# VectorE's weight halves ordered behind the recurrence's outputs while the pooling branch runs, and three of four weight sums made inside the raw tiles

## Chip, cores, metric

One core of one Trainium2 chip runs the kernel. The metric is device time in microseconds (us) of one execution: the median of 3 runs before the change was 2531.32 us (2531.08 to 2533.26). Engines are written as in the profile: PE is TensorE (PEld its weight loads), DVE is VectorE, ACT is ScalarE, POOL is GpSimd, SP is SyncE, which here only issues DMAs.

## What is computed

One layer of a hybrid trunk over 2048 positions and 1024 channels, all in float32. Cut to what matters here:

```python
xn = rmsnorm(x, norm1_g)
z = xn @ w_in                                  # columns: pool | q | forget | input | output gate | branch gates
u_pool, zq, zf, zi, zo, zg = split(z)
gates = sigmoid(zg + b_gate)
ya = pool_mixer(u_pool) @ w_pa                 # trailing-window means, windows 2, 4, 8, 16
yb = hgrn2_mixer(zq, zf, zi, zo) @ w_pb        # S_t = f_t S_(t-1) + (1 - f_t) i_t ; o_t = S_t q_t
x = x + (gates[0] * ya + gates[1] * yb) @ w_o
x = x + conv_glu_ffn(rmsnorm(x, norm2_g))      # up, causal conv of width 3, SiLU gate, down
return rmsnorm(x, final_g)
```

## The kernel before

**Stages.** The sequence is worked in two superblocks of 1024 positions, each of two blocks of 512. For each superblock the kernel runs a mixer (the projections `io`, `fq`, `u` and `g`, then the pooling branch `pa`, the recurrence branch `pb`, and `wo`) and then the feed-forward part (`up`, `dn`). The first mixer ends some 626 us into the profile, the second runs from about 1276 us.

**Products.** A matrix product over two blocks of rows is made by a seven-product scheme of the Strassen kind: a "unit" (class `Unit`, L1161) is one 2x2 arrangement of weight quarters q0 to q3, multiplied in seven products P1, P6, P5, P7, P2, P4, P3 (`ORDER`, L50). Four of them need a sum of weight quarters: `SUM_OF` (L349) names s2 for P6, s1 for P5, s3 for P7 and s4 for P3. Products gather in three PSUM banks X, Z and V. Between P6 and P7, DVE must take u2 = e1 - Z out of bank Z (L1196), since P7 adds to Z again; between P7 and P4 it must take u3 = Z - e1 (L1200) for the same reason. PE waits at P7 or at P4 when that read is late.

**Weight halves.** Each product is made of three matmuls per 128 rows with a weight tile split in two: `convert` (L216) lets ACT round the tile to float32r (L231, "high half") and DVE subtract it from the original (L232, "low half"), both into an `ops` tile. Six ops tiles exist (`N_OPS`), so the halves of product j can be written only when product j - 6 is finished. The source is a raw tile (L192), of which there are eight (`N_RAW`), filled by a DMA that SP issues (L197).

**The sums.** In the first mixer `weights_of_unit` (L433) makes each unit's four sums on POOL (L444). Each goes to a tile of its own out of the 77 slots that all stages share (`slot`, L109), and `keep` (L332) has it stored to DRAM by SP (L341). The second mixer loads the stored sums (`sums_of_unit`, L423) and makes none. So the sums are made in the first mixer alone, for the 14 units of `PROJ` (L55): fq0, g0, u0, fq1, g1, g2, fq2, g3, u1, g4, fq3, g5, g6, g7.

**The recurrence.** `hgrn_task` (L965) runs beside the projections for 4 heads and 2 blocks. At its end DVE scales the output, `ot` (L1138, four parts), PE transposes it (L1144), ACT copies it (L1146), and it goes through DRAM to become an operand of `pb`. `ot` needs a row factor `ro` from POOL (L691). The last head's outputs fall into the time of the pooling branch.

**What sets the order.** The kernel emits instructions from one Python loop: every six matmuls a tick (L136) advances one conversion and the waiting tasks. The Tile scheduler then sets the order of each engine's instructions; `behind(a, b)` (L259) adds an ordering edge between two instructions of one engine, without a wait. `quiet[0]` is true from P1 of the last unit (L1482) to the end of the `pb` branch (L1563).

Of the kernel before, what the change touches and what calls it, by code (L numbers as in the profile page):

```python
# [18 lines left out]
P = 128  # L19
# [62 lines left out]
def tile_trunk(  # L82
# [16 lines left out]
    pe, act, dve, pool, sp = nc.tensor, nc.scalar, nc.vector, nc.gpsimd, nc.sync  # L99
# [9 lines left out]
    def slot(name, cols=TB, dt=F32):  # L109
        return slots.tile([P, cols], dt, tag="s", name=name, padded_shape=[P, 528])  # L110

    def bank(name, cols=512):
        return banks.tile([P, cols], F32, tag="b", name=name, padded_shape=[P, 512])

    def f32(ap):
        return ap.bitcast(F32)
# [5 lines left out]
    class Task:  # L122
        def __init__(self, gen):
            self.gen = gen
            self.wait = 0
            self.live = True
            tasks.append(self)
# [40 lines left out]
    class Stream:  # L168
        def __init__(self):
            self.raws = []  # L170
            self.ops = []
            self.n_raw = 0
            self.tiles = []
            self.next = 0
            self.done = 0
            self.pins = {}
            self.stop = None
            self.room = LOOKAHEAD

        def raw(self, src, plus=None):  # L180
            r = Raw(src, plus)
            self.raws.append(r)
            return r
# [32 lines left out]
        def convert(self):  # L216
            j = len(self.tiles)
            key, fn, raws = self.ops[j]
            while any(r.tile is None for r in raws):
                self.load()  # L220
            for r in raws:
                r.add()
            store_kept()
            v = fn(f"w{j}")
            t = opsp.tile([P, 2, 512], F32R, tag="ops", name=f"ops{j}")
            n = int(np.prod(v.shape[1:]))
            hi, lo = t[:, 0, :n], t[:, 1, :n]
            if len(v.shape) == 3:
                hi = hi.rearrange("p (a b) -> p a b", a=v.shape[1])
                lo = lo.rearrange("p (a b) -> p a b", a=v.shape[1])  # L230
            self.mark = act.copy(hi, v)  # L231
            low = self.low = dve.tensor_tensor(lo, v, f32(hi), ALU.subtract)  # L232
            if j in self.pins:
                for ins, other in zip((self.mark, low), self.pins[j]):
                    behind(ins, other)
            self.tiles.append((key, t))
            self.load_ahead()
# [21 lines left out]
    def behind(ins, other):  # L259

        tc.add_manual_dep(ins.ins, other.ins.name, mybir.DependencyInfo(
            mybir.DependencyClass.NoSync, mybir.DependencyReason.DATA), reason="behind")
# [17 lines left out]
    stream = Stream()  # L280
# [51 lines left out]
    def keep(key, t, later=False):  # L332

        nm = "kw" + "".join(str(c) for c in np.ravel(key[1])) + f"{key[0]}{key[2]}"
        kept[key] = dram.tile([P, 512], F32, tag=nm, name=nm)
        keeping.append((kept[key], t, later))

    def store_kept():
        while keeping:
            d, t, later = keeping.pop(0)  # L340
            ins = sp.dma_start(d, t)  # L341
            if later:
                behind(ins, stream.low)
# [5 lines left out]
    SUM_OF = {"P5": "s1", "P6": "s2", "P7": "s3", "P3": "s4"}  # L349
# [42 lines left out]
    def plan_unit(key, src, kind, i, order, b0):  # L392
        mv, mg = proj_tiles(kind, i)
        if b0:
            unit = sums_of_unit(src, mv, mg, lambda p: lambda: kept["in", (kind, i), SUM_OF[p]])
        else:
            unit = weights_of_unit(src[mv], src[mg], (kind, i))
        for p in order:
            fn, raws = unit[p]()
            stream.op(key, fn, raws)  # L400
# [19 lines left out]
    def quarters(src_v, src_g):  # L420
        return [s[:, c * 512 : (c + 1) * 512] for s in (src_v, src_g) for c in range(2)]
# [10 lines left out]

    def weights_of_unit(src_v, src_g, unit):  # L433
        src = quarters(src_v, src_g)
        raws, tmp = {}, {}

        def raw(i):
            if i not in raws:
                raws[i] = stream.raw(src[i])
            return raws[i]  # L440

        def comb(nm, key, x0, x1):
            t = slot(f"{nm}{key}")
            pool.tensor_tensor(t, x0, x1, ALU.add)  # L444
            tmp[key] = t
            keep(("in", unit, key), t)
            return t

        def plan(p):
            if p == "P5":  # L450
                return (lambda nm: tmp["s1"]), []
            rs = [raw(i) for i in {"P1": (0,), "P2": (1,), "P4": (3,), "P6": (0, 2, 3),
                                   "P7": (0, 2), "P3": (1,)}[p]]

            def fn(nm):
                t = [r.tile for r in rs]
                if p == "P6":
                    comb(nm, "s1", t[1], t[2])
                    return comb(nm, "s2", tmp["s1"], t[0])
                if p == "P7":  # L460
                    return comb(nm, "s3", t[1], t[0])
                if p == "P3":
                    return comb(nm, "s4", tmp["s2"], t[0])
                return t[0]

            return fn, rs

        return {p: (lambda p=p: plan(p)) for p in ORDER}

    def up_order():  # L470
# [40 lines left out]
    prep, quiet = [], [False]  # L511
# [176 lines left out]
    def rstd_of(ssq, n, scale, name):  # L688
        r = small.tile([P, 4], F32, tag="rstd", name=name)
        pool.tensor_scalar(r[:, :n], ssq, scale, EPS, ALU.mult, ALU.add)  # L690
        pool.tensor_tensor(r[:, :n], r[:, :n], neghalf[:, :n], ALU.pow)  # L691
        return r
# [272 lines left out]
    def hgrn_task(b, h, d, q, vd, zd, od):  # L965
        def head_of(src, key):
# [14 lines left out]
        q1, q2 = (slot(f"q{i}{b}_{h}").rearrange("p (c s x) -> p c s x", c=NT, s=2)  # L981
                  for i in (1, 2))
# [68 lines left out]
        for lv in (0, 1, 2, 4, 6):  # L1051
# [35 lines left out]
            q3 = q.rearrange("p (b t h) -> p b t h", t=2, h=hh)  # L1087
# [34 lines left out]
        po = bank(f"po{b}_{h}")  # L1122
# [11 lines left out]
        r = rstd_of(so, NT, 1.0 / P, f"ro{b}_{h}")  # L1134
        yield 4
        ot = slot(f"ot{b}_{h}")
        for c in range(NT):
            dve.scalar_tensor_tensor(ot[:, c * P : (c + 1) * P], po[:, c * P : (c + 1) * P],  # L1138
                                     r[:, c : c + 1], zt[:, c * P : (c + 1) * P],
                                     ALU.mult, ALU.mult)  # L1140
        yield 4
# [3 lines left out]
        t = slot(f"oh{b}_{h}")  # L1145
# [221 lines left out]
    def mixer(b0, forms, late):  # L1367
# [16 lines left out]
        def runner():  # L1384
            while taken[0] < 2 * HEADS:
                if queue:
                    taken[0] += 1
                    yield from hgrn_task(*queue.pop(0))
                else:
                    yield 1  # L1390
# [487 lines left out]
```

## Time and profile before

| | |
|---|---|
| median of 3 runs | 2531.32 us (2531.08 to 2533.26) |
| the profiled execution, its own time | 2530.39 us |
| its span, first to last instruction | 2528.7 us |
| mean granted PE clock | 0.999 |
| busy: PE, DVE, ACT, POOL | 2507.8, 1963.1, 1195.1, 746.3 us |

The span is 1.7 us shorter than the execution's own time. Rows of the profile name an instruction by engine, line of the kernel, operation and tiles as out<-in without buffer numbers: `ops<-raw` is a weight half made from a raw tile, `gr_Z` is bank Z of a gate unit, `fr_` and `ur_` those of the forget/query and pooling units, `gr_u` a u2 or u3. Rows of time begin with the start in us from the span's start and the duration in us; a bracket at the end is the engine's idle time before the row and what ended it. In a row of a stretch each engine has its busy time and its number of instructions.

### The profile page before, as it was taken

The numbers are of one execution on the slowest core, as the hardware profiler recorded it, in microseconds if no ns is written. First come the engines' busy times: TensorE is split into PE (matmuls) and PEld (weight loads), VectorE is DVE, ScalarE is ACT, GpSimd is POOL, SyncE is SP. The second block draws the span as 40 slices with busy tenths as digits, with TensorE's granted clock in tenths as the row PEclk, the third lists the DMA queues.
The fourth block names the chain that finished last, engine by engine and source line by source line (L and its number), as shares of the span: only waits on it lengthen the run. The fifth ranks groups of instructions, "written<-read, shape, count | busy, mean of one in ns | idle before, by whom it ended". The sixth has DMA issues, their size and how long they took to land.

```text
span 2528.7 us, 35641 instructions
## 1 busy us (share of the span) xinstructions
PE 2507.8 (99%) x11508; PEld 2053.8 (81%) x11508; DVE 1963.1 (78%) x3476; ACT 1195.1 (47%) x2250; POOL 746.3 (30%) x1127
## 2 busy tenths in 40 slices
PE   9999999999999999999999999999999999999998
PEld 7888888788888888888888888888888888888887
DVE  7788878598898777885596778665979988778755
ACT  6534443334555454554554444542355554445534
POOL 4333453003354334451320202200033432325410
PEclk9999999999999999999999999999999999999999
DMA  8877777777898879997344343447443454447852
GB/s 272 271 184 231 203 203 231 221 230 244 200 259 231 229 230 240 265 364 244 123 150 150 109 134 109 138 148 233 140 155 118 151 153 135 153 133 245 321 166 97
DMA packets 252331, 493.75 MB, mean 195 GB/s; under 512 B 26544, under 2 KB 43056, under 8 KB 251824
## 3 DMA queue, kind: packets, MB, share of 16 engines
q1 hardware_dynamic: 184512, 313.60, 39.2%
q0 software_dynamic: 42656, 112.74, 17.5%
q10 hardware_dynamic: 24976, 65.13, 7.5%
q8 instruction: 91, 1.49, 0.2%
q14 instruction: 96, 0.79, 0.1%
HBM read 381.79 MB, written 187.17 MB: 225 GB/s over the span
## 4 chain that ended last, share of the span: by engine, by line
PE 92%; DVE 3%; DMA 1%; ACT 1%; issue 1%; POOL 0%; SPq 0%; ACTq 0%; DVEq 0%; POOLq 0%
PE dn_P L148 16%; PE up_Z L148 15%; PE up_V L148 10%; PE up_X L148 10%; PE wo_P L148 6%; PE gr_Z L148 4%; PE pb L148 4%; PE pa L148 3%; PE gr_X L148 3%; PE io_Z L148 3%; PE gr_V L148 3%; PE fr_Z L148 2%; PE io_V L148 2%; PE fr_X L148 2%; PE fr_V L148 1%; PE pl L1026 1%
## 5 line engine op out<-in xcount | busy, mean ns | idle before, releaser
L231 ACT CAST ops<-raw 128x512 fp32r<-128x512 f32 x744 | 459.6, 621 | 816.0 <-PE dn_P L148 179.5
L232 DVE TENSOR_TENSOR ops<-raw,ops 128x512 fp32r<-128x512 f32 x744 | 555.3, 750 | 216.7 <-ACT ops L231 209.8
L1614 DVE SCALAR_TENSOR_TENSOR e<-h,cols,e 128x512 f32<-128x512 f32 x176 | 143.3, 819 | 31.0 <-ACT e L1612 25.4
L1612 ACT ACTIVATE e<-h,cols 128x512 f32<-128x512 f32 x176 | 142.2, 814 | 25.1 <-DVE h L1159 18.3
L1617 DVE SCALAR_TENSOR_TENSOR e<-h,cols,e 128x512 f32<-128x512 f32 x176 | 133.9, 770 | 2.5
L961 POOL DMA_DIRECT2D g_P<-dg_P x154 | 84.0, 547 | 159.8 <-PE dn_P L148 111.3
L1269 POOL TENSOR_TENSOR gf_P<-e,e 128x512 f32<-128x512 f32 x44 | 61.2, 1392 | 149.4 <-DVE e L1623 95.9
L1269 POOL TENSOR_TENSOR gf_P<-gf_P,e 128x512 f32<-128x512 f32 x44 | 59.3, 1347 | 71.9 <-DVE e L1623 71.5
L1409 POOL TENSOR_TENSOR q<-q,qs 128x512 f32<-128x512 f32 x16 | 21.6, 1347 | 187.5 <-ACT qs L1408 180.3
L1607 POOL COPY h<-h 128x2 f32<-128x2 f32 x88 | 39.9, 466 | 117.7 <-DVE h L1158 113.6
L1621 ACT ACTIVATE e<-e 128x512 f32<-128x512 f32 x88 | 55.6, 632 | 38.3 <-DVE e L1617 38.0
L1446 ACT ACTIVATE gt<-gt,cols 128x512 f32<-128x512 f32 x48 | 34.8, 725 | 79.5 <-DVE gt L1159 47.1
L1609 POOL COPY hist<-h 128x2 f32<-128x2 f32 x88 | 35.5, 404 | 117.9 <-DVE h L1159 116.1
L1159 DVE TENSOR_TENSOR h<-up_u,up_V 128x512 f32<-128x512 f32 x88 | 60.1, 683 | 10.3 <-PE up_V L148 9.8
L1244 DVE TENSOR_TENSOR x<-x,wo_P 128x512 f32<-128x512 f32 x88 | 56.0, 681 | 12.1 <-PE wo_P L148 11.9
L1244 DVE TENSOR_TENSOR ac<-ac,dn_P 128x512 f32<-128x512 f32 x72 | 47.1, 681 | 16.7 <-PE dn_P L148 16.5
L1011 POOL COPY qm<-q 128x64 f32<-128x64 f32 x64 | 26.2, 437 | 96.9 <-DVE q L1043 18.2
L1637 POOL DMA_DIRECT2D dg_P<-gf_P x88 | 50.8, 577 | 8.1 <-POOL gf_P L1269 7.4
L1194 ACT COPY up_e<-up_X 128x512 f32<-128x512 f32 x44 | 25.8, 587 | 57.7 <-PE up_X L148 52.6
L1607 POOL COPY h<-hist 128x2 f32<-128x2 f32 x88 | 44.2, 510 | 27.4 <-DVE m_T42l L657 27.3
L1026 PE MATMUL pl<-qm,k 128*128 128x192 f32 x256 | 50.6, 326 | 1.0 <-DVE at L1037 0.9
L1026 PEld LDWEIGHTS pl<-qm,k 128*128 128x128 f32 x256 | 44.0, 189 | 6.2 <-POOL u L925 1.2
(1285 smaller groups left out, 8084.9 us busy)
## 6 DMA issues: line engine op xcount, KB each, us to landing
g_P<-dg_P POOLq DMA_DIRECT2D x154, 256.0 KB, 6.0
raw<-in_w_up_t SPq DMA_DIRECT2D x132, 256.0 KB, 3.3
raw<-in_w_in_t SPq DMA_DIRECT2D x98, 256.0 KB, 3.4
dg_P<-gf_P POOLq DMA_DIRECT2D x88, 256.0 KB, 3.9
dg_P<-e SPq DMA_DIRECT2D x66, 256.0 KB, 3.5
raw<-in_w_dn SPq DMA_DIRECT2D x66, 256.0 KB, 3.6
x<-in_x SPq DMA_DIRECT2D x64, 256.0 KB, 4.6
gd<-gt ACTq DMA_DIRECT2D x64, 256.0 KB, 3.2
```

The source lines that it names most:

```text
L148: count[1] = pe.matmul(*args, **kw)
L231: self.mark = act.copy(hi, v)
L232: low = self.low = dve.tensor_tensor(lo, v, f32(hi), ALU.subtract)
L961: eng.dma_start(t, d)
L1026: ins = pe.matmul(pa_[:, c * 192 : c * 192 + 192], ks[:, (i + c) * P : (i + c + 1) * P], mv[:, c].rearrange("p s x -> p (s x)"), start=Tru ...
L1159: return dve.tensor_tensor(dst, t, ps, ALU.add if how == "add" else ALU.subtract)
L1244: dve.tensor_tensor(t, t, ps[j], ALU.add if sg > 0 else ALU.subtract)
L1269: pin(eng.tensor_tensor(t, x0, x1, op))
L1607: pool.tensor_copy(h[:, 0:2], hist[:, mt] if hf == 0 else hs[s, 0][:, TB : TB + 2])
L1612: in_turn(act.activation(t, h[:, 2:], AF.Identity, bias=col(o_cb + mt), scale=col(o_cw + 4 * MF + mt)))
L1614: in_turn(second(dve.scalar_tensor_tensor(t, h[:, 1 : 1 + TB], col(o_cw + 2 * MF + mt), t, ALU.mult, ALU.add)))
L1617: dve.scalar_tensor_tensor(t, h[:, 0:TB], col(o_cw + mt), t, ALU.mult, ALU.add)
```

## The change

Two edits.

First, `convert` puts DVE's low half behind the latest `ot` output on DVE (`stream.front`, the fourth part of the last `ot` that was emitted) whenever `quiet[0]` is true. This is an order on DVE, not a wait on another engine.

Second, three of a unit's four sums lose their slots. s3 = q0 + q2 is written over q0, s1 = q2 + q3 over q2, and s4 = s2 + q1 over q1; only s2 = s3 + q3 still has a slot. P6's step now emits three sums (s3, s2, s1) and P7's none. Since q0 is overwritten, the sum s3 must follow P1's halves, which read q0; likewise s4 must follow P2's. The stores of s1, s3 and s4 read the raw tiles, so the next load into such a tile follows its store. There are still four sums and four stores a unit.

```diff
@@ -175,6 +175,7 @@
             self.done = 0
             self.pins = {}
             self.stop = None
+            self.front = None
             self.room = LOOKAHEAD
 
         def raw(self, src, plus=None):
@@ -230,6 +231,8 @@
                 lo = lo.rearrange("p (a b) -> p a b", a=v.shape[1])
             self.mark = act.copy(hi, v)
             low = self.low = dve.tensor_tensor(lo, v, f32(hi), ALU.subtract)
+            if quiet[0] and self.front is not None:
+                behind(low, self.front)
             if j in self.pins:
                 for ins, other in zip((self.mark, low), self.pins[j]):
                     behind(ins, other)
@@ -432,36 +435,35 @@
 
     def weights_of_unit(src_v, src_g, unit):
         src = quarters(src_v, src_g)
-        raws, tmp = {}, {}
+        raws, made = {}, {}
 
         def raw(i):
             if i not in raws:
                 raws[i] = stream.raw(src[i])
             return raws[i]
 
-        def comb(nm, key, x0, x1):
-            t = slot(f"{nm}{key}")
+        def comb(key, t, x0, x1):
             pool.tensor_tensor(t, x0, x1, ALU.add)
-            tmp[key] = t
-            keep(("in", unit, key), t)
+            made[key] = t
             return t
 
         def plan(p):
-            if p == "P5":
-                return (lambda nm: tmp["s1"]), []
-            rs = [raw(i) for i in {"P1": (0,), "P2": (1,), "P4": (3,), "P6": (0, 2, 3),
-                                   "P7": (0, 2), "P3": (1,)}[p]]
+            rs = [raw(i) for i in {"P1": (0,), "P6": (0, 2, 3), "P5": (2,), "P7": (0,),
+                                   "P2": (1,), "P4": (3,), "P3": (1,)}[p]]
 
             def fn(nm):
-                t = [r.tile for r in rs]
                 if p == "P6":
-                    comb(nm, "s1", t[1], t[2])
-                    return comb(nm, "s2", tmp["s1"], t[0])
-                if p == "P7":
-                    return comb(nm, "s3", t[1], t[0])
+                    q0, q2, q3 = (r.tile for r in rs)
+                    comb("s3", q0, q0, q2)
+                    comb("s2", slot(f"{nm}s2"), q0, q3)
+                    comb("s1", q2, q2, q3)
                 if p == "P3":
-                    return comb(nm, "s4", tmp["s2"], t[0])
-                return t[0]
+                    comb("s4", rs[0].tile, made["s2"], rs[0].tile)
+                if p not in SUM_OF:
+                    return rs[0].tile
+                t = made[SUM_OF[p]]
+                keep(("in", unit, SUM_OF[p]), t)
+                return t
 
             return fn, rs
 
@@ -1135,7 +1137,8 @@
         yield 4
         ot = slot(f"ot{b}_{h}")
         for c in range(NT):
-            dve.scalar_tensor_tensor(ot[:, c * P : (c + 1) * P], po[:, c * P : (c + 1) * P],
+            stream.front = dve.scalar_tensor_tensor(
+                                     ot[:, c * P : (c + 1) * P], po[:, c * P : (c + 1) * P],
                                      r[:, c : c + 1], zt[:, c * P : (c + 1) * P],
                                      ALU.mult, ALU.mult)
         yield 4
```

How this moves instructions is seen on two engines. In the changed kernel the line numbers are 2 or 3 higher, and the sum's line is L446. The names are those of the program: `w114s1` is the slot with s1 for op 114, `raw85` to `raw88` are the raw tiles of unit g6 with q0, q2, q3, q1, and numbers behind the last underscore are buffers.

POOL, around the sums of unit g6, before:

```order
L444 TENSOR_TENSOR w112s4_4181<-w107s2_3997,raw84_3662 128x512
L304 DMA su2s3_3476<-in_w_up_t 512x1x512
L444 TENSOR_TENSOR w114s1_4235<-raw86_3814,raw87_3892 128x512
L444 TENSOR_TENSOR w114s2_4238<-w114s1_4235,raw85_3812 128x512
L1011 COPY qm0_3_4_0_4280<-q0_3_4050 128x2x8x4
L1011 COPY qm0_3_4_2_4286<-q0_3_4050 128x2x8x4
L1011 COPY qm1_3_4_0_4297<-q1_3_3983 128x2x8x4
L1011 COPY qm1_3_4_2_4303<-q1_3_3983 128x2x8x4
L444 TENSOR_TENSOR w116s3_4326<-raw86_3814,raw85_3812 128x512
```

and in the changed kernel:

```order
L446 TENSOR_TENSOR raw84_3632<-w107s2_3962,raw84_3632 128x512
L978 MEMSET at1_3_4076 128x512
L307 DMA su2s3_3449<-in_w_up_t 512x1x512
L446 TENSOR_TENSOR raw85_3780<-raw85_3780,raw86_3782 128x512
L446 TENSOR_TENSOR raw86_3782<-raw86_3782,raw87_3860 128x512
L446 TENSOR_TENSOR w114s2_4200<-raw85_3780,raw87_3860 128x512
L1013 COPY qm0_3_4_0_4243<-q0_3_4016 128x2x8x4
L1013 COPY qm0_3_4_2_4249<-q0_3_4016 128x2x8x4
```

Before, s1 and s2 stand ahead of the recurrence's copies and s3 behind them; now s3, s1 and s2 stand in a row, and s3 reads and writes `raw85`, which P1's halves (op 113) read first.

DVE, around u2 of unit g5 (`gr0_5_u2`) and the low half of g6's P1 (`ops113`), before:

```order
L1073 COPY_PREDICATED at0_3_4097<-md0_1178,pl0_3_1_4162 128x256
L1086 COPY_PREDICATED at0_3_4097<-m1_917,pl0_3_1_4162 128x256
L1094 TENSOR_TENSOR k0_3_4094<-k0_3_4094,f0_3_4017 128x256
L1096 TENSOR_TENSOR f1_3_4077<-f1_3_4077 128x256
L1196 TENSOR_TENSOR gr0_5_u2_4172<-gr0_5_e1_4134,gr0_5_Z_4136 128x512
L1073 COPY_PREDICATED at1_3_4111<-md0_1178,pl1_3_1_4167 128x256
L1086 COPY_PREDICATED at1_3_4111<-m1_917,pl1_3_1_4167 128x256
L1094 TENSOR_TENSOR k1_3_4108<-k1_3_4108,f1_3_4077 128x256
L1092 TENSOR_TENSOR q0_3_4050<-q0_3_4050,f0_3_4017 128x128x2
L1092 TENSOR_TENSOR q1_3_3983<-q1_3_3983,f1_3_4077 128x128x2
L232 TENSOR_TENSOR ops112_4184<-w112s4_4181,ops112_4184 128x512
L232 TENSOR_TENSOR ops113_4212<-raw85_3812,ops113_4212 128x512
```

and in the changed kernel:

```order
L1098 TENSOR_TENSOR f1_3_4042<-f1_3_4042 128x256
L233 TENSOR_TENSOR ops111_4108<-raw83_3608,ops111_4108 128x512
L1094 TENSOR_TENSOR q1_3_3950<-q1_3_3950,f1_3_4042 128x128x2
L1199 TENSOR_TENSOR gr0_5_u2_4137<-gr0_5_e1_4099,gr0_5_Z_4101 128x512
L1098 TENSOR_TENSOR f1_3_4042<-f1_3_4042 128x128
L1075 COPY_PREDICATED at0_3_4062<-md0_1178,pl0_3_1_4127 128x256
L1088 COPY_PREDICATED at0_3_4062<-m1_917,pl0_3_1_4127 128x256
L233 TENSOR_TENSOR ops112_4148<-raw84_3632,ops112_4148 128x512
L1096 TENSOR_TENSOR k0_3_4059<-k0_3_4059,f0_3_3983 128x256
L233 TENSOR_TENSOR ops113_4176<-raw85_3780,ops113_4176 128x512
```

In both, `ops113` stands behind u2. The rows L1073, L1086 and L1094 (now L1075, L1088 and L1096) stood ahead of u2 and now stand behind it.

DVE, around the last output `ot1_3` of the first mixer (`ya` are the gated sums of the pooling branch, `ops133` and `ops134` low halves for `pb`), before:

```order
L657 TENSOR_TENSOR mxs1_3l_4891<-mx1_3_4888,mxs1_3h_4890 128x512
L1519 TENSOR_TENSOR ya0_0_4924<-gl0_0_0_4894,pa0_0_4906 128x512
L232 TENSOR_TENSOR ops133_5014<-raw99_4660,ops133_5014 128x512
L232 TENSOR_TENSOR ops134_5053<-raw100_4689,ops134_5053 128x512
L1138 SCALAR_TENSOR_TENSOR ot1_3_4957<-po1_3_4859,ro1_3_4874,z1_3_4787 128x128 x4
L1519 TENSOR_TENSOR ya0_4_4962<-gl0_0_4_4898,pa0_4_4930 128x512
L1517 SCALAR_TENSOR_TENSOR ya1_0_4977<-gl1_0_0_4896,pa1_0_4964 128x512
```

and in the changed kernel:

```order
L659 TENSOR_TENSOR mxs1_3l_4849<-mx1_3_4846,mxs1_3h_4848 128x512
L1522 TENSOR_TENSOR ya0_0_4882<-gl0_0_0_4852,pa0_0_4864 128x512
L1140 SCALAR_TENSOR_TENSOR ot1_3_4915<-po1_3_4817,ro1_3_4832,z1_3_4745 128x128 x4
L1522 TENSOR_TENSOR ya0_4_4920<-gl0_0_4_4856,pa0_4_4888 128x512
L1520 SCALAR_TENSOR_TENSOR ya1_0_4935<-gl1_0_0_4854,pa1_0_4922 128x512
L233 TENSOR_TENSOR ops133_4972<-raw99_4619,ops133_4972 128x512
L233 TENSOR_TENSOR ops134_5011<-raw100_4647,ops134_5011 128x512
```

The two low halves went from ahead of `ot1_3` to behind it and behind two rows of the pooling branch.

## The prediction

> **What bounds the kernel now.** I read the page's busy times first, then two stretches side by side: the projections of the first mixer (97.70 to 454.29 us, where all the sums are made) and the same projections of the second mixer (1357.40 to 1703.76 us, where none is). In a stretch's row the columns are the bounds, the length, then busy time and count for PE, PEld, DVE, ACT and POOL.
>
> ```profile
> PE 2507.8 (99%) x11508; PEld 2053.8 (81%) x11508; DVE 1963.1 (78%) x3476; ACT 1195.1 (47%) x2250; POOL 746.3 (30%) x1127
> 97.70:454.29 356.59, 350.89 (x1777) 292.37 (x1776) 288.10 (x663) 151.92 (x335) 138.84 (x151) 1.00 0.77 218
> 1357.40:1703.76 346.36, 346.36 (x1770) 291.13 (x1769) 252.53 (x651) 153.82 (x334) 56.56 (x86) 1.00 0.43 129
> ```
>
> PE is busy for 99% of the span, so only PE's idle time is to be had. The second mixer's projections leave PE no idle time at all; the first's leave 356.59 - 350.89 = 5.70 us and take 10.2 us more. The rest of those 10.2 us is work that only the first stretch holds (seven matmuls more) and steps too short to count as idle. In the first mixer POOL is busy 138.84 instead of 56.56 us and DVE 288.10 instead of 252.53 us, for nearly the same work. Next I read PE's rows in time and kept those with idle time ahead of them, from there to the end of the pooling branch:
>
> ```profile
> 154.30 0.89 PE L1026 MATMUL pl<-qm,k 128*128 128x192 f32 x4 [0.91 <-DVE at L1037]
> 206.71 0.50 PE L148 MATMUL gr_Z<-x_T30h,ops 128*128 128x512 f32 x1 [0.92 <-DVE gr_u L1196]
> 283.14 0.50 PE L148 MATMUL gr_Z<-x_T30h,ops 128*128 128x512 f32 x1 [0.32 <-DVE gr_u L1196]
> 311.63 0.50 PE L148 MATMUL ur_Z<-x_T30h,ops 128*128 128x512 f32 x1 [1.79 <-DVE ur_u L1196]
> 362.54 0.50 PE L148 MATMUL fr_Z<-x_T30h,ops 128*128 128x512 f32 x1 [0.26 <-DVE fr_u L1196]
> 387.08 0.51 PE L148 MATMUL gr_Z<-x_T30h,ops 128*128 128x512 f32 x1 [0.95 <-DVE gr_u L1196]
> 413.67 0.50 PE L148 MATMUL gr_Z<-x_T30h,ops 128*128 128x512 f32 x1 [0.46 <-DVE gr_u L1196]
> 466.08 0.33 PE L1144 MATMUL pt<-ident,ot 128*128 128x128 f32 x1 [1.83 <-DVE ot L1138]
> ```
>
> The brackets sum to 7.44 us, and DVE ends every one: six times it is u2, once the recurrence, once the last output `ot`. So the change is worth what it does to DVE's lateness at these eight places, plus any new place.
>
> **Why DVE is late: the sums.** DVE's rows and POOL's rows at the wait of 387.08 (u2 of unit g5):
>
> ```profile
> 381.87 0.41 DVE L1096 TENSOR_TENSOR f<-f 128x256 f32<-128x256 f32 x1
> ...
> 383.64 1.35 DVE L1094 TENSOR_TENSOR k<-k,f 128x256 f32<-128x256 f32 x1
> 384.91 1.51 DVE L1096 TENSOR_TENSOR f<-f 128x256 f32<-128x256 f32 x1
> 386.35 0.68 DVE L1196 TENSOR_TENSOR gr_u<-gr_e,gr_Z 128x512 f32<-128x512 f32 x1
> ...
> 388.05 0.45 DVE L1094 TENSOR_TENSOR k<-k,f 128x256 f32<-128x256 f32 x1
> ```
>
> ```profile
> 383.41 1.30 POOL L444 TENSOR_TENSOR w114s<-raw,raw 128x512 f32<-128x512 f32 x1 [0.63 <-DMA kwg5ins<-w109s]
> 384.79 1.35 POOL L444 TENSOR_TENSOR w114s<-w114s,raw 128x512 f32<-128x512 f32 x1
> ```
>
> L1094 takes 0.45 us a few rows later and 1.35 us beside the first add; L1096 takes 0.41 us before and 1.51 us beside the second. Each add holds one DVE row up by 0.9 to 1.1 us, 2.0 us in all, where PE waited 0.95. Both adds are s1 and s2 of the next unit (g6), made as soon as raw tiles and slots allow. The same at u1, and at u0 and g6:
>
> ```profile
> 306.15 1.40 DVE L1017 TENSOR_TENSOR q<-qm,f 128x128 f32<-128x128 f32 x1
> ...
> 307.67 1.25 DVE L1017 TENSOR_TENSOR q<-qm,f 128x128 f32<-128x128 f32 x1
> ...
> 311.76 0.28 DVE L1043 TENSOR_TENSOR q<-q,f 128x128 f32<-128x128 f32 x1
> ```
>
> ```profile
> 305.91 1.49 POOL L444 TENSOR_TENSOR w93s<-raw,raw 128x512 f32<-128x512 f32 x1 [1.30 <-issue]
> 307.48 1.29 POOL L444 TENSOR_TENSOR w93s<-w93s,raw 128x512 f32<-128x512 f32 x1
> ```
>
> ```profile
> 151.63 1.76 DVE L232 TENSOR_TENSOR ops<-raw,ops 128x512 fp32r<-128x512 f32 x1
> ...
> 410.80 1.17 DVE L1017 TENSOR_TENSOR q<-qm,f 128x128 f32<-128x128 f32 x1
> ```
>
> ```profile
> 151.37 1.47 POOL L444 TENSOR_TENSOR w51s<-w51s,raw 128x512 f32<-128x512 f32 x1
> ...
> 410.06 1.76 POOL L444 TENSOR_TENSOR w121s<-w121s,raw 128x512 f32<-128x512 f32 x1
> ```
>
> At u1 two rows are 1.12 and 0.97 us over the 0.28 us of that shape, 2.09 us for a wait of 1.79. At g6 it is 0.89 for 0.46. At u0 a low half takes 1.76 us (two take 1.29 us in the row quoted below), so 1.1 for 0.91.
>
> **The change, part by part.** *The sums.* s3 now waits for the low half of the next unit's P1, and s1 and s2 follow it. That low half needs an ops tile that is free only after P6 of the running unit, and the order shown has it behind u2. So the next unit's s1 and s2 can't run ahead of this u2, and the four places where they did lose their cause: -(0.95 + 1.79 + 0.91 + 0.46) = **-4.11 us**. I take each wait whole, since each stretch is longer than the wait.
>
> At 206.71 (g1) the order of DVE changes: five rows of the recurrence go behind u2, one low half (s4's product, P3) goes ahead of it. The shortest shape among the five takes about the 0.41 us of L1096 above, so some 2 us leave and 0.65 enters: **-0.92 us**, the wait. At 283.14 (g3) a low half enters ahead of u2 and nothing leaves: **+0.6 us**. 362.54 stays.
>
> *The output.* The rows before 466.08 on DVE, and `ro`, which `ot` needs, on POOL; then the same place in the second mixer, on DVE and on PE:
>
> ```profile
> 461.92 0.68 DVE L1519 TENSOR_TENSOR ya<-gl,pa 128x512 f32<-128x512 f32 x1
> 464.48 1.29 DVE L232 TENSOR_TENSOR ops<-raw,ops 128x512 fp32r<-128x512 f32 x2 [1.88 <-ACT ops L231]
> 465.69 1.12 DVE L1138 SCALAR_TENSOR_TENSOR ot<-po,ro,z 128x128 f32<-128x128 f32 x4
> ```
>
> ```profile
> 457.21 1.01 POOL L691 TENSOR_TENSOR ro<-ro,neghalf 128x4 f32<-128x4 f32 x1
> ```
>
> ```profile
> 1712.05 1.12 DVE L1138 SCALAR_TENSOR_TENSOR ot<-po,ro,z 128x128 f32<-128x128 f32 x4
> ```
>
> ```profile
> 1715.14 0.27 PE L1144 MATMUL pt<-ident,ot 128*128 128x128 f32 x1
> ```
>
> DVE idles 1.88 us for a low half while `ot` could run: `ro` was done at 458.22. Put first, `ot` starts at 462.6 and ends at 463.7, 0.5 us before PE stops at 464.25 for its first part (466.08 - 1.83). The second mixer has that order already, and its transpose waits for nothing. **-1.83 us**. The two low halves lose no time, as ACT ends their wait; what now stands ahead of them (`ot` and two `ya`) is 1.12 + 2 x 0.68 us, and their products come a branch later.
>
> *The new waits.* POOL waits for P1's low half before s3 and for P2's before s4. Behind it stand the recurrence's copies and `ro`. No row shows such a wait; the nearest are waits of the same adds for a slot, and of DVE for a slot that a stored sum still held:
>
> ```profile
> POOL w91s L444 <- DVE gt L1159: 4.1, 1, 4.1
> DVE ss L1117 <- DMA kwg4ins<-w98s: 4.2, 1, 4.2
> ```
>
> These go, since s1, s3 and s4 take no slot. So the new wait lies between +4 and -4 us of POOL time at a place; I take nothing. The loads into raw tiles now follow the stores. The row of loads and that of stores of the same size (KB each, median us to landing), and one product of PE in the chain of work:
>
> ```profile
> raw<-in_w_in_t SPq DMA_DIRECT2D x98, 256.0 KB, 3.4
> ...
> dg_P<-e SPq DMA_DIRECT2D x66, 256.0 KB, 3.5
> ```
>
> ```profile
> 106.04 2.79 PE fr_Z L148 x12
> ```
>
> A store and a load take 6.9 us; a tile is loaded more than a unit of seven products, 19.5 us, ahead. Nothing.
>
> *The three adds in a row.* They now fall behind P1's low half, before or around u3, which PE needs at P4. Between P7 and P4 lies P2 (2.79 us); u3 takes 0.69, so 2.1 us are to spare, two held-up rows. The tightest place is g4:
>
> ```profile
> 344.03 0.69 DVE L1200 TENSOR_TENSOR gr_u<-gr_Z,gr_e 128x512 f32<-128x512 f32 x1
> ```
>
> ```profile
> 344.77 0.50 PE L148 MATMUL gr_Z<-x_T40h,ops 128*128 128x512 f32 x1
> ```
>
> PE goes on 0.05 us after u3's end. Bounds: no held-up row ahead of u3 costs nothing, three (3.3 us) cost 1.2 us in each of 13 units. I take one per unit, since POOL starts s3 only after u2 and P1's low half: 1.05 us at g4, **+1.1 us**.
>
> Sum: -4.11 - 0.92 + 0.6 - 1.83 + 1.1 = -5.2 us on the profiled execution's 2530.39 us (its span 2528.7 and 1.7 around it): 2525.2. That execution lies 0.9 us under the median of the runs, so the forecast is **2526.2 us**.
>
> **The rivals.** *All the waits go.* Without slots to wait for, DVE may be early everywhere: 7.4 us of idle rows, at most about 10.4 with the short steps (10.2 less seven matmuls of 0.23, plus 1.83): 2521 to 2524. For it: the second mixer shows no wait. Against: it makes no sums, and 56 adds still hold DVE up.
>
> *The sums move less than the order says.* If u2 stays late for other reasons (a backlog, s4's add), only the output's 1.83 us and a part of the rest come: about 2529. For it: DVE is 81% busy there. Two held-up rows per unit ahead of u3 give the same: 13 x 0.1 + 2.2 at g4 = +3.5 in place of +1.1, 2528.6.
>
> *Slower: three adds ahead of u3.* If s3, s1 and s2 each hold a row between P1's low half and u3, PE waits 1.2 us in 13 units: +15.6 in place of +1.1, so 2540.7. It decides from the third held-up row on. For it: at 387 two adds in a row held two rows in a row. Against: u2 comes earlier, which moves P1's low half and the adds earlier too. The Trainium skill (SBUF — State Buffer, section "SBUF: two separate sides") has it that a DVE instruction with two SBUF inputs and a POOL one that reads SBUF exclude each other for the whole instruction, whichever starts first. By that rule alone, three adds of 1.3 us are a block of 3.9 us, 1.8 over what is spare, 23 us in all: about 2549. The rows above agree with the exclusion, but show DVE getting one row in between two adds.
>
> **How the numbers follow.** Forecast 0.38 (its own range 2524 to 2528.5), all waits gone 0.22, less than the order says 0.28, slower 0.12. The range reaches from 2521 to 2533 and leaves out the slower case. A difference under 0.2% (5.06 us, down to 2526.26) is about what a measurement of this kernel can tell from no change. The forecast lies on that bound, and I give 0.21 of its 0.38 to the far side: faster 0.43, same 0.45, slower 0.12.
>
> **What would show it.** Right: no idle ahead of the first `pt` near 464; the rows beside L446 adds stretched, but none just ahead of a u2; waits of 311 and 387 gone; no slot waits at the sums. Wrong: PE's Z matmuls waiting for u3 (now L1202 or L1203), or POOL's adds waiting long for low halves and `ro` with them. If the first mixer's projections take over 358 us, the third add decided.

## The result: 8.8 us faster, by the sums alone

| | before | after |
|---|---|---|
| median of 6 runs | 2531.94 us (2531.08 to 2533.26) | 2523.11 us (2522.01 to 2523.89) |
| the profiled execution, its own time | 2530.39 us | 2523.21 us |
| its span | 2528.7 us | 2521.5 us |

The ratio is 0.9964, with a 95% interval of 0.9951 to 0.9977: 8.8 us or 0.35% faster. That is inside the range of 2521 to 2533 and on the right side, but 3.1 us under the forecast of 2526.2, and where the rival "all the waits go" had put it (2521 to 2524). It is more than the 0.2% that the prediction took for the bound between "same" and "faster". The two profiled executions differ by 7.2 us, since that of before lay 1.6 us under its median.

The busy times of the page after, then the stretches between the same points of the program, first after, then before (a stretch begins where the projections, then `pb`, begin; the columns are as in the prediction):

```profile
PE 2507.2 (99%) x11508; PEld 2054.5 (81%) x11508; DVE 1943.1 (77%) x3476; ACT 1195.6 (47%) x2250; POOL 744.5 (30%) x1127
```

```profile
97.85:489.92 392.07, 392.07 (x1971) 328.18 (x1970) 291.84 (x698) 165.15 (x362) 144.45 (x155) 1.00 0.80 227
489.92:1348.93 859.01, 858.02 (x3766) 695.84 (x3765) 684.75 (x1012) 428.01 (x755) 287.76 (x439) 1.00 0.77 228
1348.93:1741.78 392.85, 391.89 (x1970) 327.87 (x1969) 273.20 (x688) 166.72 (x362) 55.37 (x88) 1.00 0.45 139
```

```profile
97.70:499.99 402.29, 394.75 (x1970) 327.72 (x1969) 309.18 (x700) 165.21 (x363) 141.23 (x154) 1.00 0.77 221
499.99:1357.40 857.41, 857.11 (x3766) 695.77 (x3765) 685.01 (x1012) 428.00 (x755) 286.75 (x439) 1.00 0.77 228
1357.40:1748.97 391.57, 391.57 (x1970) 327.87 (x1969) 273.52 (x688) 166.90 (x362) 57.76 (x88) 1.00 0.46 140
```

Three things are to be seen. The first mixer gained 402.29 - 392.07 = 10.2 us, and PE is now busy in all of it: all eight waits are gone. The stretch up to the second mixer lost 1.6 us and the second mixer 1.3 us, 0.96 of it idle. And DVE is busy 309.18 - 291.84 = 17.3 us less in the first mixer, with 698 rows against 700 and the same 56 adds in the kernel: it has no less to do, it is held up less. Up to `pb` both kernels have the same number of products in both mixers (1970 or 1971), so the prediction's "seven matmuls more" were order and not work.

### The profile page after: what moved, and what is told of

Same layout as the page of the kernel before. It is cut to its first block, busy times and chain, and to the rows that moved or that the text cites. A ratio compares the mean times of both kernels' runs of the same rounds, so it can differ in the third digit from the quotient of the medians.

```text
span 2521.5 us, 35651 instructions
## 1 busy us (share of the span) xinstructions
PE 2507.2 (99%) x11508; PEld 2054.5 (81%) x11508; DVE 1943.1 (77%) x3476; ACT 1195.6 (47%) x2250; POOL 744.5 (30%) x1127
## 4 chain that ended last, share of the span: by engine, by line
PE 97%; POOL 1%; DMA 1%; DVE 0%; issue 0%; ACT 0%; SPq 0%; POOLq 0%; DVEq 0%
PE dn_P L148 16%; PE up_Z L148 15%; PE up_X L148 10%; PE up_V L148 10%; PE wo_P L148 6%; PE gr_Z L148 5%; PE gr_X L148 4%; PE pb L148 4%; PE gr_V L148 3%; PE pa L148 3%; PE io_Z L148 3%; PE fr_Z L148 3%; PE fr_X L148 2%; PE io_V L148 2%; PE fr_V L148 2%; PE pl L1028 2%
## 5 line engine op out<-in xcount | busy, mean ns | idle before, releaser
L232 ACT CAST ops<-raw 128x512 fp32r<-128x512 f32 x786 | 485.5, 620 | 854.1 <-PE dn_P L148 177.7
L233 DVE TENSOR_TENSOR ops<-raw,ops 128x512 fp32r<-128x512 f32 x786 | 578.0, 738 | 225.1 <-ACT ops L232 218.8
L446 POOL TENSOR_TENSOR raw<-raw,raw 128x512 f32<-128x512 f32 x28 | 38.9, 1389 | 103.4 <-DVE ops L233 102.4
```

## Where the held-up rows went

DVE's rows at g5 after, where u2 (L1199) had been late by 0.95 us; POOL's adds at the same place; and PE's first matmul that needs u2:

```profile
377.78 0.68 DVE L1199 TENSOR_TENSOR gr_u<-gr_e,gr_Z 128x512 f32<-128x512 f32 x1
...
380.74 0.70 DVE L233 TENSOR_TENSOR ops<-raw,ops 128x512 fp32r<-128x512 f32 x1
381.34 0.76 DVE L1075 COPY_PREDICATED at<-md,pl 128x256 f32<-128x256 uint8 x1
381.86 0.83 DVE L1088 COPY_PREDICATED at<-m,pl 128x256 f32<-128x256 uint8 x1
382.45 0.66 DVE L1096 TENSOR_TENSOR k<-k,f 128x256 f32<-128x256 f32 x1
383.03 0.68 DVE L1203 TENSOR_TENSOR gr_u<-gr_Z,gr_e 128x512 f32<-128x512 f32 x1
383.74 0.69 DVE L1162 TENSOR_TENSOR gt<-gr_u,gr_V 128x512 f32<-128x512 f32 x1
```

```profile
381.52 2.73 POOL L446 TENSOR_TENSOR raw<-raw,raw 128x512 f32<-128x512 f32 x2 [7.37 <-DVE ops L233]
384.22 1.27 POOL L446 TENSOR_TENSOR w114s<-raw,raw 128x512 f32<-128x512 f32 x1
```

```profile
379.81 0.39 PE L148 MATMUL gr_Z<-x_T30h,ops 128*128 128x512 f32 x1
```

u2 ends 1.35 us before PE needs it. The three adds now follow P1's low half (380.74), behind u2. Most rows that they meet read PSUM: the mask copies (`pl` is a PSUM bank), u3 and the gate's last subtraction. These take their usual time to within 0.1 us; only one row with two SBUF operands, L1096, is held up, by 0.2 us. In before the same line (then L1094) took 1.35 us here.

How the shapes fare over the whole of the first mixer's projections after (columns: count, then the shortest, median and longest duration in ns):

```profile
L1039 DVE COPY_PREDICATED at<-m,pl x64: 276/292/306, 145.6 to 409.8; 128x128 f32<-128x128 uint8 x64
L1203 DVE TENSOR_TENSOR gr_u<-gr_Z,gr_e x8: 673/684/692, 130.5 to 434.2; 128x512 f32<-128x512 f32 x8
L1096 DVE TENSOR_TENSOR k<-k,f x24: 410/456/1257, 125.3 to 414.9; 128x256 f32<-128x256 f32 x24
```

The mask copies and u3 stay within 11% of their shortest; a row with two SBUF operands can take three times its own (the longest L1096, at 161.62, lies beside another POOL add of SBUF tiles, L936). Of the 14 rows of u3, nine lie beside a sum's add, two in before, and they take 673 to 693 ns. I laid DVE's rows over POOL's adds and took from each row that overlaps an add the duration at the 20th percentile of its shape: before, 121 rows lay beside adds and were 38.0 us too long; after, 112 rows were 17.9 us too long, 30 of them mask copies with 0.3 us in all. So as many rows meet adds as before, but they are other rows.

POOL pays for it with waits (columns: total, times, longest). PE waits for none of the sums; ACT does when it makes the high halves, 6.5 us at u0 and again at u1, against at most 4.8 in before, and that reaches PE nowhere:

```profile
POOL raw L446 <- DVE ops L233: 104.7, 18, 9.3
```

## A new wait in the second mixer

PE, DVE and SP at the second mixer's last output transposes, after:

```profile
1707.77 0.33 PE L1147 MATMUL pt<-ident,ot 128*128 128x128 f32 x1 [0.96 <-DVE ot L1140]
```

```profile
1699.21 0.86 DVE L1140 SCALAR_TENSOR_TENSOR ot<-po,ro,z 128x128 f32<-128x128 f32 x3
...
1700.58 1.29 DVE L233 TENSOR_TENSOR ops<-raw,ops 128x512 fp32r<-128x512 f32 x2
```

```profile
1706.77 0.69 DVE L1522 TENSOR_TENSOR ya<-gl,pa 128x512 f32<-128x512 f32 x1 [3.59 <-DMA gl<-gd]
1707.37 1.12 DVE L1140 SCALAR_TENSOR_TENSOR ot<-po,ro,z 128x128 f32<-128x128 f32 x4
```

```profile
1691.56 0.32 SPq L963 DMA_DIRECT2D mx<-md  x1
1701.33 0.93 SPq L198 DMA_DIRECT2D raw<-in_w_pb_t  x2
1702.36 0.42 SPq L963 DMA_DIRECT2D gl<-gd  x1
```

Read it from the end. `ot` stands behind `ya` on DVE; `ya` waits for the gate `gl`, which is reloaded from DRAM; SP issues that reload at 1702.36, behind two raw loads; those wait for raw tiles, which come free when the two low halves at 1700.58 have read them. The output edit put these two behind an `ot`, but not behind the last one: they stand behind the output before it (1699.21). In before, where the second mixer begins 8.5 us later, such a pair ran at 1699.88 and 1704.00, ahead of that output (1705.99). The prediction looked only at the next pair, the one around the last output. My first theory, then: the sums make the whole gain by the place of their adds, and the output edit costs time through SP's queue. The rivals: the freed slots make the gain; or, as the prediction had it, the output edit is worth 1.8 us.

## The experiments

Twelve kernels ran, each beside the kernel before on its chip, whose medians there lay between 2531.62 and 2532.46 us. First the two edits, with two ways to part the adds' place from the slots:

| sums | without the output edit | with it |
|---|---|---|
| as before (four slots, early) | 2531.94 us | 2541.01 us |
| in raw tiles, behind P1's low half (one slot) | 2521.43 us | 2523.11 us (the changed kernel) |
| same place, three slots | 2520.32 us | 2529.26 us |
| early, two slots | 2541.07 us | 2544.68 us |

**The output edit alone.**

```diff
+            if quiet[0] and self.front is not None:
+                behind(low, self.front)
...
-            dve.scalar_tensor_tensor(ot[:, c * P : (c + 1) * P], po[:, c * P : (c + 1) * P],
+            stream.front = dve.scalar_tensor_tensor(
```

> The kernel before with the output edit alone (low halves behind the last ot rows while the pooling branch runs; sums as before). My theory: it saves the wait of 1.83 us at the first mixer's output transposes and pays one in the second mixer, where the trace after has PE waiting 0.96 us (a step 1.12 us long) for ot: about 0.7 us faster, 0.5 to 1.9 faster at most, the eight waits of the projections unchanged. Rival (the second mixer's new wait comes from the sums, not from this edit): 1.8 us faster and no wait at the second mixer's transposes.

Measured: 2541.01 us, ratio 1.0034 (1.0021 to 1.0047): 8.9 us slower. The prediction's term and my first theory's number fall: not a gain at all. PE, DVE, POOL and SP in the first mixer's pooling branch, and the DMA issues of 455 to 472 us (columns: count, KB each, median us to landing):

```profile
471.54 0.47 PE L1148 MATMUL pt<-ident,ot 128*128 128x128 f32 x1 [6.38 <-DVE ot L1141]
```

```profile
458.61 1.29 DVE L233 TENSOR_TENSOR ops<-raw,ops 128x512 fp32r<-128x512 f32 x2
...
470.53 0.69 DVE L1523 TENSOR_TENSOR ya<-gl,pa 128x512 f32<-128x512 f32 x1 [9.33 <-DMA gl<-gd]
471.14 1.12 DVE L1141 SCALAR_TENSOR_TENSOR ot<-po,ro,z 128x128 f32<-128x128 f32 x4
```

```profile
458.69 1.24 POOL L307 DMA_DIRECT2D su2s<-in_w_up_t  x1
```

```profile
460.38 8.23 SPq L964 DMA_DIRECT2D gl<-gd  x8
```

```profile
gl<-gd SPq DMA_DIRECT2D x8, 256.0 KB, 11.3
su2s<-in_w_up_t POOLq DMA_DIRECT2D x1, 1024.0 KB, 14.0
```

The two low halves at 458.61 are again the pair behind the output before the last. In before they stand 4 and 8 us earlier:

```profile
450.62 0.69 DVE L232 TENSOR_TENSOR ops<-raw,ops 128x512 fp32r<-128x512 f32 x1 [0.84 <-ACT ops L231]
...
454.46 0.68 DVE L232 TENSOR_TENSOR ops<-raw,ops 128x512 fp32r<-128x512 f32 x1
```

The chain is the one seen in the second mixer, but the wait is 6.38 us in place of 1.83. The gates are issued at 460.38, against 456.57 before, and land late: `ya` runs 10.2 us after the issue, against 5.4 before (461.92). Between the two lies `su2s` at 458.69, a 1 MB transfer that adds weights of the next stage in DRAM. Before the change the gates were issued 1.6 us ahead of that transfer (458.18); here 1.7 us behind it. In before, too, the three gates issued just behind the transfer took 7.2 to 11.3 us to land, against 4.7 to 5.0 for the three ahead of it; here the one that `ya` waits for is among the late ones.

The wait has a second price. PE in the 6.83 us for which its granted clock was lower, and in a stretch of the same kind behind it (the column after POOL's is the granted clock):

```profile
470.39:477.22 6.83, 5.68 (x14) 4.54 (x15) 4.86 (x11) 0.00 (x0) 0.00 (x0) 0.50 0.85 314
477.30:484.00 6.70, 6.70 (x32) 5.49 (x31) 2.59 (x4) 1.31 (x2) 0.00 (x0) 1.00 0.80 267
```

PE is busy for 5.68 us of it at half the clock, which is 2.8 us of its work. In before and in the changed kernel the granted clock is full from the projections to PE's last product. Of the 8.9 us, 6.38 - 1.83 = 4.6 are the wait here, 2.8 the clock behind it and 1.4 the second mixer's transposes; longer waits at u0 and g1, which the edit doesn't touch, add 1.2, and g6's wait of 0.46 is gone.

**The sums alone.** The changed kernel without the two lines in `convert`.

> The changed kernel without the output edit: the sums alone. My theory: nearly the whole gain, 7 to 9 us faster than before, no wait at the second mixer's output transposes; the wait of 1.83 us at the first mixer's transposes may stay, which gives 7, or go since DVE is held up less, which gives 9. Rival (as the prediction had it, the sums are worth 3.4 us and the rest is the output edit and its order): 3 to 4 us faster.

Measured: 2521.43 us, ratio 0.9958 (0.9945 to 0.9970): 10.7 us faster than before, more than with the output edit. PE is never idle from the projections to `pb`, the output transposes included:

```profile
97.70:489.60 391.90, 391.90 (x1971) 328.45 (x1970) 292.92 (x699) 165.23 (x362) 143.10 (x155) 1.00 0.80 227
```

So the sums are the whole gain, and they also remove the 1.83 us that the output edit was made out to be worth: DVE has the last `ot` (453.34) ahead of the two low halves (457.15) without being told.

**Early adds, and three slots, both with the output edit.** The first takes the wait for P1's low half away, by a slot for s3; the second keeps that wait but gives s1 and s4 slots again (s1 is ordered behind s2 on POOL).

```diff
-                    comb("s3", q0, q0, q2)
-                    comb("s2", slot(f"{nm}s2"), q0, q3)
-                    comb("s1", q2, q2, q3)
+                    comb("s3", slot(f"{nm}s3"), q0, q2)
+                    comb("s1", q2, q2, q3)
+                    comb("s2", slot(f"{nm}s2"), q2, q0)
```

```diff
-                    comb("s1", q2, q2, q3)
+                    comb("s1", slot(f"{nm}s1"), q2, q3)
...
-                    comb("s4", rs[0].tile, made["s2"], rs[0].tile)
+                    comb("s4", slot(f"{nm}s4"), made["s2"], rs[0].tile)
```

> The changed kernel with s3 in a slot of its own again, so that s3, s1 and s2 need no low half and may run as soon as their raw tiles are there; two slots for each unit's sums, where the kernel before had four and the changed one has one. Theory 1 (the place of the adds among DVE's rows decides): most of the gain is lost, 0 to 4 us faster than before, DVE's rows beside the adds stretched as before (some 38 us in the first mixer, against 18 us after). Theory 2 (the freed slots decide): most of the gain stays, 6 to 9 us faster.

> The changed kernel with the sums' place kept (s3 in its raw tile behind P1's low half, s2 and s1 after it) but s1, s2 and s4 in slots: three slots for each unit, where the kernel before had four and the changed one has one. Theory 1 (the place of the adds decides): the gain stays, 7 to 9 us faster than before. Theory 2 (the freed slots decide): 0 to 4 us faster, with DVE and POOL waiting for slots that stored sums hold.

Measured: early adds 2544.68 us, ratio 1.0052 (1.0038 to 1.0065), 12.6 us slower than before although half of the slots are freed; rows beside adds 34.9 us too long. Three slots 2529.26 us, 0.9988 (0.9979 to 0.9997), 2.8 us faster. The first speaks for the place. The second lies between the two theories' numbers, but its trace parts them: of the eight waits one of 0.2 us is left in the projections, and a wait of 5.4 us for `ot` (1.83 before) stands in the pooling branch, with the gates issued at 450.86 and `su2s` at 449.17, again 1.7 us behind, and again 6.83 us at a clock of 0.50. So both were tried again without the output edit.

**The same two without the output edit.**

> The three-slot kernel (s3 in its raw tile behind P1's low half; s1, s2 and s4 in slots) without the output edit. If the adds' place alone makes the gain in the projections and the 5.4 us wait of the three-slot kernel belongs to the output edit: as the sums alone, 2521 to 2523 us. If three slots in place of one cost time of their own: 2525 to 2530.

> The kernel with the three adds early (s3 in a slot, none of the three waits for a low half) without the output edit. If the adds' place decides, the loss against the sums alone is in the projections and stays: 2536 to 2542 us, PE waiting for u2 as long as with the output edit (some 15 us over the first mixer). If its loss was mostly the output edit's: 2522 to 2530.

Measured: three slots 2520.32 us, ratio 0.9956 (0.9943 to 0.9968); early adds 2541.07 us, 1.0037 (1.0025 to 1.0050). With the adds in their new place, one slot or three makes no difference to the time, though with three PE waits 0.76 us at g1 (205.19); with the adds early, the kernel is 9.5 us slower than before. The place decides, and the slots don't. PE's waits with early adds (columns as above), then DVE and POOL ahead of the 3.7 us wait at u0:

```profile
PE gr_Z L148 <- DVE gr_u L1197: 6.0, 3, 3.8
PE ur_Z L148 <- DVE ur_u L1197: 3.7, 1, 3.7
PE fr_Z L148 <- DVE fr_u L1197: 1.9, 1, 1.9
```

```profile
149.93 2.63 DVE L1015 TENSOR_TENSOR qm<-qm,f 128x128 f32<-128x128 f32 x2
152.49 1.26 DVE L1045 TENSOR_TENSOR f<-f 128x8 f32<-128x8 f32 x1
153.68 0.28 DVE L1034 COPY_PREDICATED at<-m,pl 128x128 f32<-128x128 uint8 x1
153.88 1.60 DVE L1047 TENSOR_TENSOR k<-k,f 128x384 f32<-128x384 f32 x1
...
157.76 0.67 DVE L1197 TENSOR_TENSOR ur_u<-ur_e,ur_Z 128x512 f32<-128x512 f32 x1
```

```profile
150.40 1.81 POOL L444 TENSOR_TENSOR w51s<-raw,raw 128x512 f32<-128x512 f32 x1
152.28 1.44 POOL L444 TENSOR_TENSOR raw<-raw,raw 128x512 f32<-128x512 f32 x1
153.80 1.27 POOL L444 TENSOR_TENSOR w51s<-raw,raw 128x512 f32<-128x512 f32 x1
```

Three adds in a row hold one SBUF row each, all ahead of u2; the mask copy among them takes its 0.28 us. In before two adds ran ahead of u2 in a row; here it is three, and the waits are longer. Behind three of them (at u0, at the 1.9 us of `fr_Z` and at the 3.8 us of `gr_Z`) the granted clock is 0.50 for 3.41 us, together 4.8 us of PE's work. So this kernel is slower than before and not equal to it.

**No adds at all.** In the sums alone, `comb` makes no add and hands its first operand on, so most products have other weights and the result is not the layer's.

```diff
-            pool.tensor_tensor(t, x0, x1, ALU.add)
-            made[key] = t
-            return t
+            made[key] = x0
+            return x0
...
-                    comb("s2", slot(f"{nm}s2"), q0, q3)
+                    comb("s2", q0, q0, q3)
...
-                    comb("s4", rs[0].tile, made["s2"], rs[0].tile)
+                    comb("s4", rs[0].tile, rs[0].tile, made["s2"])
```

> The sums alone, with the 56 adds left out (the products take raw tiles in place of the sums, and the stores keep raw tiles, so the weights of most products are others). If the moved adds still hold DVE up where PE waits: 1 to 5 us faster than the sums alone. If nothing of their cost is left on the path: within 0.5 us of it, though DVE loses its 18 us of stretched rows.

Measured: 2520.83 us, ratio 0.9957 (0.9943 to 0.9971). PE is as busy from the projections to `pb` as with the adds, though DVE is busy 16.7 us less and POOL 70.7 us less:

```profile
97.70:489.60 391.90, 391.90 (x1972) 328.33 (x1971) 276.21 (x697) 167.85 (x362) 72.45 (x102) 1.00 0.79 225
```

So in their new place nothing of the adds' cost is left on PE's path.

**Why the output edit costs 8.9 us alone: queue or collision.** The output edit alone, twice more: with the gates reloaded through POOL's queue, and with the preparing transfers held back from the third-last unit until after the branch.

```diff
-                gates[s, m, hf] = fetch(gd[s, m, hf], f"gl{b0 + hf}_{s}_{m}")
+                gates[s, m, hf] = fetch(gd[s, m, hf], f"gl{b0 + hf}_{s}_{m}",
+                                          sp if s else pool)
```

```diff
-            while quiet[0]:
+            while quiet[0] or hold[0]:
...
+                if n == len(PROJ) - 3 and p == "P7":
+                    hold[0] = True
```

> The output edit alone, as in the first run of that edit, with the pooling branch's gates reloaded through POOL's queue instead of SP's. Theory 1 (the moved low halves free their raw tiles late, SP's raw loads wait for those, and the gates behind them on SP's queue make ya late, with ot behind ya on DVE): the wait for ot falls from 6.4 us to under 2 in the first mixer and the one of 1.4 in the second goes; 2530 to 2535 us. Theory 2 (ot is late for the low halves' or the DMA engines' sake whatever the queue): the wait stays at 5 us or more, 2539 to 2543.

> The output edit alone, gates on SP's queue as in the first run of that edit, but the 1 MB transfers that prepare the next layer's sums are held back from the last two units until after the pooling branch. Theory 1 (SP's queue: the gates are issued late behind raw loads, and that alone makes ya and ot late): the gates are still issued near 460 us on SP and the wait for ot stays at 5 to 6.5 us in the first mixer. Theory 3 (the gates, issued after a 1 MB transfer in place of before it, land in 10 us in place of 5): the gates land in 3 to 6 us and the wait falls under 2 us; the second mixer, which prepares no sums, keeps its 1.4 us. The total may carry other costs of the later transfers, so the wait decides.

Measured: gates on POOL's queue 2529.89 us, ratio 0.9994 (0.9986 to 1.0003), both waits for `ot` gone; held back 2535.28 us, 1.0013 (1.0004 to 1.0022), runs from 2532.07 to 2539.27. The first alone doesn't part the two theories, since on POOL's queue the gates also moved ahead of `su2s`. The second does. SP, DVE and the DMA issues of 455 to 472 us there:

```profile
459.16 4.05 SPq L964 DMA_DIRECT2D gl<-gd  x8
```

```profile
463.57 0.69 DVE L1525 TENSOR_TENSOR ya<-gl,pa 128x512 f32<-128x512 f32 x1 [3.54 <-DMA gl<-gd]
```

```profile
gl<-gd SPq DMA_DIRECT2D x12, 256.0 KB, 5.0
```

The gates are still issued late on SP, but `ya` runs 4.4 us later and PE's first-mixer wait is gone: without the transfer the edit does save the 1.83 us that the prediction gave it. In the second mixer, where no sums are prepared, the new wait stays, at 1.33 us. So there are two mechanisms. The late issue on SP's queue costs PE about 1 us in the second mixer (1.37 alone, 0.96 in the changed kernel, 0.20 with three slots) and by itself nothing in the first. In the first, the gates slip behind the 1 MB transfer as well, and that is the wait of 6.4 us and the lower clock behind it. What else the held-back transfers cost, and why this kernel scatters over 7 us, was not followed.

**The changed kernel's own give-back.** Both edits with the gates on POOL's queue; then the changed kernel with the output edit in the first mixer only, beside the changed kernel once more.

```diff
-            if quiet[0] and self.front is not None:
+            if quiet[0] and self.front is not None and not self.late:
...
+                    stream.late = b0 > 0
```

> The changed kernel (both edits) with the pooling branch's gates reloaded through POOL's queue. If the second mixer's wait of 0.96 us for ot is due to the gates behind raw loads on SP's queue: that wait goes and the kernel comes to the sums alone, 2520.5 to 2522 us. If it has another cause: the wait stays, 2522.5 to 2524.

> The changed kernel with the output edit in the first mixer only. If the edit's cost in the changed kernel is the second mixer's wait of 0.96 us for ot: that wait is gone and the time lies 0.7 to 2 us under the changed kernel run beside it, as the sums alone did (2521 to 2522 us). If the edit costs nothing in the changed kernel and the sums alone were lower by scatter: within 0.5 us of the changed kernel beside it.

> The changed kernel once more, beside the one with the output edit in the first mixer only, so that the two share a chip: 2522 to 2524 us, with the second mixer's wait of about 1 us for ot.

Measured: gates on POOL's queue 2522.21 us (2521.37 to 2524.40), ratio 0.9959 (0.9946 to 0.9971): the second mixer's wait is gone, but one of 0.45 us for ACT's half of `mxs` comes up in the first, and the time alone decides nothing. First mixer only 2521.68 us (2521.20 to 2522.47); the changed kernel beside it 2523.43 us (2521.54 to 2523.60). PE there, in the second mixer:

```profile
1707.37 0.33 PE L1147 MATMUL pt<-ident,ot 128*128 128x128 f32 x1 [0.99 <-DVE ot L1140]
```

With the edit in the first mixer only this wait is gone and the median lies 1.75 us lower, as with the sums alone. About 1 us of that is the wait shown; the rest is inside the scatter. The sums alone, with one slot or three, have lower medians than both kernels.

## Why the prediction was right, and where it was not

- **PE bound by eight late DVE rows:** right. All eight went, and the first mixer gained 10.2 us, 7.4 of idle rows and the rest in steps too short to count as idle.
- **"The next unit's s1 and s2 can't run ahead of this u2", -4.11 us:** right. Three slots keep all four waits away, so slots had no part in it. Early adds bring waits back, larger, at g5 (3.84 us for 0.95) and u0 (3.68 for 0.91), and new ones elsewhere; those at u1 and g6 don't come back, and why was not followed.
- **g1, -0.92 us:** the wait is gone, but its cause stays open: three slots, with the adds in the new place, wait 0.76 us there, and early adds don't.
- **g3, +0.6 us; 362.54 "stays":** wrong in size. At g3 u2 ends at 280.25, 0.1 us before PE needs it, and the wait at 362.54 is gone too. I take these waits for DVE's arrears from rows held up earlier, 20 us fewer now; no run tells them apart.
- **Three adds in a row, +1.1 us:** wrong in size; nothing. I priced the rows beside those adds like the rows beside before's adds, at 0.9 to 1.1 us each. But around P1's low half DVE works for the most part on mask copies, u3 and gate subtractions, which read PSUM and were not held up. Where a row was held up ahead of u3 (L1094 at g3, 1.51 us), the spare time took it: u3 ends at 286.55, 1.7 us ahead of PE (288.22). At g4 u3 now ends at 337.02, 2.6 us ahead of PE (339.61), where it had 0.05.
- **The output, -1.83 us:** this step failed. "The two low halves lose no time [...] and their products come a branch later" looked at the pair around the last output, and not at the pair before it, which the edit moved too (from 450.62 and 454.46 to 458.61); and it looked at what the halves are for, not at what they free: raw tiles, for which SP's next loads wait, with the gates behind them on SP's queue, and `ya` and `ot` behind the gates on DVE. Alone it costs 8.9 us. In the changed kernel it costs about 1: the gates are still issued at 448.59, 0.17 us ahead of the 1 MB transfer at 448.76, and the second mixer pays 0.96 us. "The second mixer has that order already" was true of the pair around its last output, and not of the pair before it (1699.88 and 1704.00).
- **POOL's new waits, 0:** right in effect, though they add up to 104.7 us, up to 9.3 at a time, where I had bounded them by 4. **Loads behind stores, 0:** right, by the sums alone.
- **The slower rival** (2540.7): its mechanism is real, and early adds show it, three adds holding three rows, but at u2. After P1's low half it did not come about, for the rows there. The strict rule gave 2549. As the Trainium skill states it (SBUF — State Buffer, section "SBUF: two separate sides"), the rule bears, outside DVE's 2-port modes, only on DVE instructions with two SBUF inputs. The trace agrees: all nine u3 rows beside an add, with one input in PSUM, took 673 to 693 ns. I had applied the rule to such rows.
- **The sum:** -5.2 us came out where the sums alone give -10.7 and the output edit takes 1.7 of that back. That the forecast still lies only 3.1 us off is luck in part: it gave 1.83 us of gain to the edit that costs, and 1.7 us of cost to the sums that had none. The 1.6 us lost between the mixers is in part a wait of PE for normalized rows near 1258 us: 0.88 us in the profiled execution of the changed kernel and 0.26 in that of its second measurement, so scatter; the rest was not located.

## What to carry to other kernels

Where two engines hold each other up, ask which of the rows an operation will meet, not how many: moving an add by a few microseconds from rows with two SBUF operands to rows that read PSUM freed 20 us of DVE without taking any work away. When a step is moved later, follow what it releases: the buffer, the load that waits for it, and everything behind that load in its queue. And a transfer with microseconds to spare is not safe if a large one is issued next to it: 1.7 us on the wrong side of a 1 MB transfer cost 5 to 6 us, and the wait that came of it another 2 to 3 us of lower clock. So read the granted clock behind every long wait that a change brings.

## What the hardware showed that was not expected

- DVE rows with a PSUM operand run at full speed beside a POOL add of SBUF tiles: in the changed kernel the 30 mask copies of 128x128 beside such an add took 281 to 305 ns (276 to 306 elsewhere) and the nine u3 rows 673 to 693 ns, while a row with two SBUF operands reached 1257 ns beside a POOL add from a median of 456.
- Reloads of 256 KB issued just behind a 1 MB transfer that adds in DRAM, issued by POOL, took 11.3 us (the output edit alone) in place of 5.0 (the same with that transfer held back; medians of their stretches). Those issued ahead of it were not slowed: 4.7 to 5.0 us in before.
- After a PE wait of 6.4 us, and again of 5.4, the granted clock was 0.50 for 6.83 us; after 3.7 and 3.8 us with early adds, for 3.41. Near 1.9 us it came either way: the wait of 1.92 us at fq3 was followed by it in the execution of early adds alone, and not in that of early adds with the output edit.
